# One gather of 256 columns for the first two expert pairs of a layer, in place of two of 128

## The chip, the cores and the metric

The kernel runs on one NeuronCore of a Trainium2 chip. The metric is device time in microseconds (us) of one execution, the median of several. The engines are TensorE (matmuls, "PE"; its weight loads are shown apart as "PEld"), VectorE ("DVE"), ScalarE ("ACT"), GpSimdE ("POOL") and SyncE ("SP"), whose queue issues the DMAs that bring the weights.

## What is computed

The reference is a transformer of two layers over 256 tokens of `x` and 256 tokens of context, width 1024. Each layer has a mixer (a gated recurrence and spatial gating in layer 0, latent attention in layer 1) and then a mixture of 32 experts, of which each token takes two. Layer 0 sends 512 tokens to its experts, layer 1 only the 256 of `x`. For each expert:

```
g, u = split(xb @ w_gu[e])          # xb: the rows of the tokens that chose e; w_gu 1024 x 1024
y    = (silu(g) * u) @ w_dn[e]      # w_dn 512 x 1024
out[token] += weight[token, e] * y
```

## The kernel before

Everything that the change touches is in `moe`, which runs once in each layer. An expert has 64 places (`CAP`), and two experts make a pair, so a layer has 16 pairs; `step(p)` does one pair. Tokens are brought to places by matmuls with one-hot matrices. `one_hots(g)` makes, in one VectorE instruction, the matrix `P` for two pairs at once: 256 columns, the first 128 for the even pair and the last 128 for the odd one. `gather` (L871) multiplies the token rows, kept as a high and a low part in fp32r, by `P`: for each of 8 blocks of 128 features it issues one matmul for each token tile and part. That is 8 x 8 = 64 matmuls in layer 0 (`NT` = 4 token tiles) and 8 x 4 = 32 in layer 1 (`NT` = 2), each with as many columns as the `P` that it was given. The products land in PSUM tiles named `ad` (3 buffers of 512 columns: 4 blocks at 128 columns, 2 at 256) and ACT and DVE copy them to `xT`.

The order of TensorE's work in the expert loop is that of the source (`manual_schedule`). In `step(p)` it is: `gate_up` of the first expert and of the second (L916, 64 matmul records in a step, of 512 columns in fp32, two of them side by side in the array), then a filler, then `turned` (L935, transposes of the hidden rows), then the rest of the filler, `back` (L901, transposes of the weights of the places) and `down` (L1027, 32 records). Between the last matmul of `gate_up` and `turned` stands `hidden` (L920), a chain of ACT and DVE instructions; the filler is what TensorE does meanwhile. It is:

- for an odd pair: the gather of the next two pairs, of 256 columns;
- for a later even pair: `combine` (L1046), which adds the results of the pairs before to the tokens;
- for pair 0: the gather of the second half of `P`, 128 columns, that pair 1 will need. The first half was gathered ahead of the loop, and `R.blocks` (L309, some tiny matmuls) follows it.

After pair 11 of layer 0 and pair 5 of layer 1 (`MID`) all results so far are combined and every engine takes a branch (`tc.If`, L1179) round a loop for overfull experts. The step after it, an even one, finds nothing to combine: its filler is empty.

Each pair needs 12 loads of 1 MB, issued by SP in order (`load_to`, L849) into a ring of 13 buffers in layer 0 and 17 in layer 1. A load waits until the matmuls that read the old content of its buffer are done. The ring is full when a layer's first gather starts.

Of the kernel before, what the change touches and what calls it, by code (L numbers as in the profile page):

```python
# [25 lines left out]
def body(ctx, tc, I, out, dbg=None, stop=None):  # L26
# [783 lines left out]
    def moe(R, wxa, nwb, out=None):  # L810
# [5 lines left out]
        with ExitStack() as st:  # L816
# [16 lines left out]
            def load_to(n):  # L833

                for i in range(len(loads), min(n, n_load)):
                    p, j = divmod(i, 12)
                    e, j, src = (2 * p + j // 4, j % 4, I["moe_w_gu"]) if j < 8 else (2 * p + (j - 8) // 2, j % 2, I["moe_w_dn"])
                    w = turn[i % len(turn)].tile([128, 2, D], F32, name="w")
                    if i >= n_load - 4:

                        c = (i - n_load + 4) // 2
                        v = w.rearrange("p k (h n) -> p (k h) n", h=2)
                        for e in range(2):
                            nc.sync.dma_start(v[:, 2 * e:2 * e + 2],
                                              src[l, NE - 2 + e, j * 256:(j + 1) * 256, c * 512:(c + 1) * 512]
                                              .rearrange("(p k) n -> p k n", p=128))
                        loads.append(v)
                        continue
                    nc.sync.dma_start(w, src[l, e, j * 256:(j + 1) * 256, :].rearrange("(p k) n -> p k n", p=128))  # L849
                    loads.append(w)  # L850
# [10 lines left out]
            def weigh(P, b, weights):  # L861

                a = weights.shape[2]
                n = 128 // a
                Pw = mo.tile([128, NT, 128], F32, name="z", bufs=4)
                V.tensor_tensor(Pw.rearrange("p t (a n) -> p t a n", a=a),
                                P[:, :, 128 * b:128 * b + 128].bitcast(F32).rearrange("p t (a n) -> p t a n", a=a),
                                weights[:, :, :, None].to_broadcast([128, NT, a, n]), op=OP.mult)
                return Pw

            def gather(P, xT, q0=0, q1=4):  # L871

                n = P.shape[2]
                m = 512 // n
                for cb in range(2 * q0 // m, 2 * q1 // m):
                    px = Q("ad", (128, m, n))
                    for j in range(m):
                        k = cb * m + j
                        for i in range(2 * NT):
                            t, part = divmod(i, 2)  # L880
                            mm(px[:, j, :], hs[t][:, part, 256 * (k // 2) + k % 2:256 * (k // 2) + 256:2], P[:, t, :],  # L881
                               start=i == 0, stop=i == 2 * NT - 1)
                    if R.mod is None:
                        if cb % 2:
                            act(xT[:, cb * m:cb * m + m], px, AF.Copy)
                        else:
                            V.tensor_copy(xT[:, cb * m:cb * m + m], px)
                        continue
                    for j in range(m):
                        k = cb * m + j  # L890
                        S, A = [R.mod[:, g, k:k + 1] for g in range(2)]
                        if j % 2:
                            act(xT[:, k], px[:, j], AF.Identity, scale=A, bias=S)
                        else:
                            V.tensor_scalar(xT[:, k], px[:, j], A, S, op0=OP.mult, op1=OP.add)

            def back(Pw):

                pt = Q("bt", (128, 4, 128))
                for t in range(NT):  # L900
                    tp(pt[:, t, :], Pw[:, t, :], ident)  # L901
                ws = mo.tile([128, 1], F32, name="ws", bufs=2)
                act(junk_of(NT * 128), pt[:, 0:NT, :].rearrange("p t n -> p (t n)"), AF.Copy, accum_out=ws)
                PT = mo.tile([128, NT, 128], F32R, name="PT", bufs=2)
                V.tensor_scalar(PT, pt[:, 0:NT, :], 0.0, None, op0=OP.is_gt)
                return PT, ws

            def gate_up(xT, base, wg):

                gu = Q("gu")  # L910
                for j in range(4):
                    w_ = wg(j)
                    for k in (2 * j, 2 * j + 1):
                        w = w_[:, k % 2, :].rearrange("p (a c n) -> p c a n", a=2, c=2)
                        for c in range(2):
                            mm(gu[64 * c:64 * c + 64, :], xT[:, k, base:base + CAP], w[:, c],  # L916
                               start=k == 0, stop=k == KC - 1)
                return hidden(gu)
# [37 lines left out]
            def total(z, t, c, pend):  # L956

                mm(z, ident, xs[t][:, c * 512:(c + 1) * 512], start=True, stop=False, skip_group_check=True)  # L958
                for y, PT in pend:
                    for part in range(2):  # L960
                        mm(z, PT[:, t, :], y[c][:, part], start=False, stop=False, skip_group_check=True)  # L961
# [150 lines left out]
            def one_hots(g):  # L1112
                return onehots(cm[:, :, 4 * g:4 * g + 4], iota[:, 0:CAP])

            def rows_tile():
                return mo.tile([128, 8, 256], F32, name="xT", bufs=1)

            def step(p):

                nonlocal xT, P  # L1120
                load_to(12 * p + 12)
                w = loads[12 * p:12 * p + 12]
                odd = p % 2
                more = odd and p < last
                b = 128 * odd
                Pw = weigh(P, odd, wsel[:, :, 2 * p:2 * p + 2])
                if more:
                    P = one_hots((p + 1) // 2)
                end = p == last and out is not None
                h = [gate_up(xT, b, lambda j: w[j])]  # L1130
                if end:
                    z = [[None] * 2 for _ in range(2)]
                    for c, t in ((0, 0), (0, 1), (1, 0)):
                        z[t][c] = Q("ad")
                        total(z[t][c], t, c, pend)
                    PT, ws = back(Pw)
                h.append(gate_up(xT, b + CAP, lambda j: w[4 + j]))
                n = 2 * NT
                if more:
                    xT = rows_tile()  # L1140
                    gather(P, xT, 0, 3)
                elif end:
                    z[1][1] = Q("gu")
                    total(z[1][1], 1, 1, pend)
                elif p == 0:
                    gather(P[:, :, 128:256], xT[:, :, 128:256])
                else:
                    combine(pend, 0, n - 1)
                hT = turned(h)
                if end:  # L1150
                    finish(hT, w[8:], PT, ws, fg, z)
                    return
                if more:
                    gather(P, xT, 3, 4)
                else:
                    combine(pend, n - 1, n)
                    pend.clear()
                PT, ws = back(Pw)
                if p < last:
                    gated = p == last - 1 and out is not None  # L1160
                    pend.append((down(hT, lambda j: (w[8 + j], w[10 + j]), ws, gated), PT))
                else:
                    settle(hT, w[8:], PT, ws)

            P = one_hots(0)
            with tc.manual_schedule(engines=pes):
                xT = rows_tile()
                gather(P[:, :, 0:128], xT[:, :, 0:128])
                R.blocks(mo, Q)
                for p in range(MID[l] + 1):  # L1170
                    step(p)
                combine(pend)
                pend.clear()
# [253 lines left out]
    with ExitStack() as main:  # L1427
        HL = main.enter_context(tc.tile_pool(name="hl", bufs=1))
        wst, wxa, R = even_layer(HL, main)
        if stop != "even":  # L1430
            moe(R, wxa, 4)
        wst.close()
# [3 lines left out]
    with ExitStack() as main:  # L1436
        HL = main.enter_context(tc.tile_pool(name="hl1", bufs=1, side="right", reuse_waits="tile"))
        R = odd_layer(HL, main)
        moe(R, wxa, 4, out)
# [40 lines left out]
```

## Time and profile before

| | |
|---|---|
| median of 3 runs | 1553.11 us (1551.04 to 1554.37) |
| the profiled execution | 1554.18 us, its span 1552.4 us |
| PE busy | 1459.8 us (94%) |
| DVE, ACT, POOL busy | 664.9, 434.0, 225.3 us |
| mean granted TensorE clock | 0.966 of full speed |
| moved by DMA | 495.24 MB, 319 GB/s over the span |

The durations of the rows below come from the profiled execution. The span runs from the first to the last instruction, and 1.8 us of the execution lie around it. The clock is given as a share of 2.4 GHz: 1.00 is 2.4 GHz and 0.50 is 1.2 GHz; a mean between the two says which share of a stretch was at which.

### The profile page before, as it was taken

The page shows a single profiled execution, that of the slowest core. Times are in us where ns is not written, and L with a number is a line of the kernel's source. Part 1 is how long each engine was busy: PE and PEld are TensorE (multiplying, and loading weights), DVE is VectorE, ACT ScalarE, POOL GpSimd, SP SyncE. Part 2 cuts the span into 40 slices and gives each one's busy share as a digit, 9 for nine tenths or more (in the row PEclk, how much of TensorE's full clock was granted, in tenths as well). Part 3 has the DMA queues.
Part 4 walks back from the last instruction along what each step waited for, and adds up shares of the span by engine and source line. Part 5 has one row for each costly group of instructions (what it writes and reads, how often), then busy time and mean ns, then how long its engine had stood idle before and what let it go on. Part 6 is the DMA issues. An engine that isn't in the chain of part 4 may idle for free. (4 is left out here: it accounts for less than half of the span.)

```text
span 1552.4 us, 21816 instructions
## 1 busy us (share of the span) xinstructions
PE 1459.8 (94%) x8622; PEld 857.8 (55%) x8622; DVE 664.9 (43%) x1498; ACT 434.0 (28%) x988; POOL 225.3 (15%) x250
## 2 busy tenths in 40 slices
PE   7999999998999999999999988997999989989987
PEld 5777777867644554554535356786344434444443
DVE  4555556758224334244413455576232332322222
ACT  4433334623121121111112144453222212212212
POOL 2321212133002112012203221101010100010010
PEclk9999999998799999999999989997999999999999
DMA  9774434885899999999999853125999999999994
GB/s 356 232 256 143 156 120 161 299 318 192 320 372 420 420 420 420 420 420 420 382 376 382 321 216 112 43 96 204 372 420 420 420 419 421 420 420 421 420 420 191
DMA packets 126052, 495.24 MB, mean 319 GB/s; under 512 B 17739, under 2 KB 38636, under 8 KB 77816
## 3 DMA queue, kind: packets, MB, share of 16 engines
q1 hardware_dynamic: 119704, 487.33, 79.6%
q10 hardware_dynamic: 2192, 3.72, 0.7%
q0 software_dynamic: 4048, 2.73, 0.6%
q8 instruction: 71, 1.16, 0.3%
q14 instruction: 37, 0.30, 0.1%
HBM read 492.59 MB, written 1.13 MB: 318 GB/s over the span
## 5 line engine op out<-in xcount | busy, mean ns | idle before, releaser
L916 PE MATMUL gu<-w,xT 128*64 128x512 f32 x2048 | 462.9, 604 | 18.0 <-DMA w<-in_moe_w_gu_dram 13.2
L916 PEld LDWEIGHTS gu<-w,xT 128*64 128x64 f32 x2048 | 153.3, 139 | 316.9 <-issue 278.5
L1027 PE MATMUL dn<-w,hh 128*64 128x512 f32 x960 | 219.5, 604 | 0.0
L924 DVE COPY hh<-gu 128x256 f32<-128x256 f32 x64 | 27.2, 425 | 371.3 <-ACT junk L923 371.3
L1050 POOL TENSOR_TENSOR xx<-xx,z 128x512 f32<-128x512 f32 x56 | 72.9, 1324 | 767.4 <-DVE z L1049 767.4
L1027 PEld LDWEIGHTS dn<-w,hh 128*64 128x64 f32 x960 | 76.1, 139 | 121.9 <-issue 112.3
L923 ACT ACTIVATE junk<-gu 128x256 f32<-128x256 f32 x64 | 24.6, 384 | 401.7 <-PE gu L916 401.7
L120 PE MATMUL mm<-WH,hH 128*128 128x512 f32 x288 | 116.7, 407 | 0.8 <-ACT hH L115 0.7
L121 PE MATMUL mm<-WL,hH 128*128 128x512 f32 x288 | 115.2, 400 | 1.4 <-DVE WL L116 1.4
L122 PE MATMUL mm<-WH,hL 128*128 128x512 f32 x288 | 112.5, 400 | 0.0
L1017 DVE SCALAR_TENSOR_TENSOR y<-dn,ws,y 128x512 fp32r<-128x512 f32 x60 | 45.0, 751 | 145.7 <-ACT y L1016 143.6
L1046 PE MATMUL ad<-y,PT 128*128 128x512 f32 x368 | 94.8, 404 | 5.3 <-DVE z L1049 4.1
L1016 ACT ACTIVATE y<-dn,ws 128x512 fp32r<-128x512 f32 x60 | 41.2, 687 | 176.1 <-PE dn L1027 165.6
L1046 PEld LDWEIGHTS ad<-y,PT 128*128 128x128 f32 x368 | 66.0, 188 | 36.1 <-issue 13.0
L115 ACT ACTIVATE WH<-w 128x512 fp32r<-128x512 f32 x80 | 48.4, 627 | 107.6 <-PE mm L122 86.0
L116 DVE TENSOR_TENSOR WL<-w,WH 128x512 fp32r<-128x512 f32 x76 | 56.6, 752 | 50.9 <-ACT WH L115 49.4
L1049 DVE TENSOR_TENSOR z<-ad,gt 128x512 f32<-128x512 f32 x100 | 66.1, 683 | 13.3 <-PE ad L1046 10.2
L881 PE MATMUL ad<-P,hH 128*128 128x256 f32 (+1 forms) x288 | 63.0, 302 | 1.5 <-DVE P L856 1.5
L120 PEld LDWEIGHTS mm<-WH,hH 128*128 128x128 f32 x288 | 54.9, 191 | 16.9 <-issue 3.8
L399 PE MATMUL ad<-w,cst 128*32 128x128 f32 x1536 | 59.3, 280 | 5.1 <-DMA w<-in_ada_w_dram 5.0
L121 PEld LDWEIGHTS mm<-WL,hH 128*128 128x128 f32 x288 | 54.8, 190 | 13.1 <-DVE WL L116 1.5
L122 PEld LDWEIGHTS mm<-WH,hL 128*128 128x128 f32 x288 | 54.5, 191 | 13.2 <-issue 1.6
(434 smaller groups left out, 1989.3 us busy)
## 6 DMA issues: line engine op xcount, KB each, us to landing
w<-in_moe_w_gu_dram SPq DMA_DIRECT2D x256, 1024.0 KB, 16.3
w<-in_moe_w_dn_dram SPq DMA_DIRECT2D x120, 1024.0 KB, 12.0
w<-in_ada_w_dram SPq DMA_DIRECT2D x48, 1024.0 KB, 7.4
w<-in_ev_w_in_dram SPq DMA_DIRECT2D x32, 256.0 KB, 4.6
w<-in_moe_w_dn_dram SPq DMA_DIRECT2D x16, 512.0 KB, 11.2
w<-in_ev_w_in_dram SPq DMA_DIRECT2D x6, 1024.0 KB, 5.1
w<-in_ev_w_out_dram SPq DMA_DIRECT2D x4, 1024.0 KB, 6.8
w<-in_od_w_out_dram SPq DMA_DIRECT2D x4, 1024.0 KB, 5.0
```

The lines of the kernel that those rows point to most:

```text
L115: act(H, src, AF.Copy)
L116: (eng or V).tensor_tensor(L, src, H, op=OP.subtract)
L120: mm(out, lh, rh, start=start, stop=False, skip_group_check=True)
L121: mm(out, lh, rl, start=False, stop=False, skip_group_check=True)
L122: return mm(out, ll, rh, start=False, stop=stop, skip_group_check=True)
L399: mm(pa[32 * j:32 * j + 32, 0:128], cst[:, k, :], w[k // 4][:, k % 4, j * 128:(j + 1) * 128], start=k == 0, stop=cols is not None and k == ...
L881: mm(px[:, j, :], hs[t][:, part, 256 * (k // 2) + k % 2:256 * (k // 2) + 256:2], P[:, t, :], start=i == 0, stop=i == 2 * NT - 1)
L916: mm(gu[64 * c:64 * c + 64, :], xT[:, k, base:base + CAP], w[:, c], start=k == 0, stop=k == KC - 1)
L1027: mm(py[c][64 * par:64 * par + 64, :], hT[par][:, k // 2, k % 2, :], w_[par][:, k % 2, c * 512:(c + 1) * 512], start=k == 0, stop=k == 3)
L1046: mm(cb, PT[:, t, :], y[c][:, i % 2], start=i == 0, stop=i == 2 * len(pend) - 1)
L1049: V.tensor_tensor(z, cb, gate[t // 2][:, hs_], op=OP.mult)
L1050: (V if n % 4 == 3 else nc.gpsimd).tensor_tensor(xs[t][:, hs_], xs[t][:, hs_], z, op=OP.add)
```

## The change

The first gather of a layer now takes the whole of `P`: as many matmuls as one of the two gathers before, each with 256 columns. The gather in pair 0's step goes. As `pend` is empty there, the `combine` that now stands in its branch does nothing, and pair 0's filler is empty.

```diff
@@ in step(p)
                 elif end:
                     z[1][1] = Q("gu")
                     total(z[1][1], 1, 1, pend)
-                elif p == 0:
-                    gather(P[:, :, 128:256], xT[:, :, 128:256])
                 else:
                     combine(pend, 0, n - 1)
                 hT = turned(h)
@@ ahead of the loop
             P = one_hots(0)
             with tc.manual_schedule(engines=pes):
                 xT = rows_tile()
-                gather(P[:, :, 0:128], xT[:, :, 0:128])
+                gather(P, xT)
                 R.blocks(mo, Q)
                 for p in range(MID[l] + 1):
                     step(p)
```

## Rows read from the trace of the kernel before

**Rows 1.** Stretches: length, busy us of PE, PEld, DVE, ACT, POOL; clock, DMA share, GB/s.

```profile
400.00:440.00 40.00, 39.25 (x213) 20.24 (x214) 9.17 (x19) 6.31 (x14) 0.00 (x0) 0.94 0.73 289
440.00:760.00 320.00, 318.62 (x1664) 159.64 (x1658) 118.28 (x195) 62.17 (x143) 40.93 (x30) 1.00 1.01 420
1108.00:1114.00 6.00, 6.00 (x30) 2.01 (x28) 0.85 (x2) 1.37 (x2) 0.00 (x0) 1.00 0.81 306
1114.00:1500.00 386.00, 364.11 (x1738) 163.50 (x1736) 113.18 (x234) 81.64 (x194) 27.45 (x21) 0.99 1.01 420
```

**Rows 2.** PE's waits, 402 to 892 us (all): us in total, times, longest.

```profile
PE ad L1046 <- DVE z L1049: 4.1, 10, 1.2
PE gu L916 <- DVEq L1179: 2.2, 1, 2.2
PE bt L935 <- DVE hh L927: 2.1, 1, 2.1
PE bt L901 <- ACT hh L939: 1.5, 2, 0.7
```

**Rows 3.** Timeline of PE, layer 0, pair 0: start, us, instructions [idle before].

```profile
402.69 15.09 PE L916 MATMUL gu<-w,xT 128*64 128x512 f32 x64
417.70 0.45 PE L881 MATMUL ad<-P,hH 128*128 128x128 f32 x2
...
427.34 7.09 PE L1027 MATMUL dn<-w,hh 128*64 128x512 f32 x32
434.26 3.17 PE L916 MATMUL gu<-w,xT 128*64 128x512 f32 x14
```

**Rows 4.** Stretches, the gather's matmuls (L881) alone: PE busy, clock, DMA.

```profile
388.69:402.43 13.74, 13.73 (x64) 0.50 0.75 310
417.70:425.30 7.60, 7.60 (x64) 1.00 1.01 423
744.63:750.51 5.88, 5.88 (x48) 1.00 1.01 417
1077.37:1084.26 6.89, 6.89 (x32) 0.50 0.06 20
```

**Rows 5.** Stretches of three `gate_up` pairs (pairs 0 and 12; layer 1, pair 0).

```profile
402.69:417.70 15.01, 15.01 (x67) 4.70 (x64) 2.99 (x9) 1.78 (x4) 0.00 (x0) 0.92 0.73 267
771.13:787.94 16.81, 16.81 (x64) 5.62 (x64) 4.58 (x8) 1.22 (x3) 0.84 (x1) 0.82 0.97 365
1084.47:1099.93 15.46, 15.46 (x67) 4.80 (x65) 3.53 (x11) 2.13 (x5) 0.00 (x0) 0.90 0.68 278
```

**Rows 6.** Timeline of PE, layer 0, pair 11 of pairs 0 to 15.

```profile
730.79 13.90 PE L916 MATMUL gu<-w,xT 128*64 128x512 f32 x64
744.63 0.52 PE L881 MATMUL ad<-P,hH 128*128 128x256 f32 x2
```

**Rows 7.** Timeline of PE, the two steps with an empty filler.

```profile
787.94 0.51 PE L935 MATMUL bt<-ident,hh 128*128 128x128 f32 x2
...
802.12 13.90 PE L916 MATMUL gu<-w,xT 128*64 128x512 f32 x64
...
1264.01 0.51 PE L935 MATMUL bt<-ident,hh 128*128 128x128 f32 x2
...
1268.18 8.78 PE L1027 MATMUL dn<-w,hh 128*64 128x512 f32 x32
1276.80 13.90 PE L916 MATMUL gu<-w,xT 128*64 128x512 f32 x64
```

**Rows 8.** Loads issued from 700 to 714 us, and us from issue to landing.

```profile
L849 SPq DMA_DIRECT2D w<-in_moe_w_gu_dram x8: 327/328/383, 701.7 to 713.3; - x8
...
DMA to landing us min/median/max: 14.8/15.9/17.9
```

**Rows 9.** Timeline of SP, layer 1: the first loads after the stop.

```profile
1088.03 3.76 SPq L849 DMA_DIRECT2D w<-in_moe_w_gu_dram  x3
```

**Rows 10.** Timeline of PE, layer 1, pair 0.

```profile
1105.97 7.09 PE L1027 MATMUL dn<-w,hh 128*64 128x512 f32 x32
```

## The prediction

> **What bounds the kernel now.** I read the slices first, to see which stage is bound by what, then the waits of TensorE, then the timeline round the first gather, and last the clock of each stretch. The expert loops of the two layers have different bounds.
>
> In layer 0 TensorE is the bound. From 440 to 760 us it is busy for 318.62 of 320.00 us, and the DMA engines are busy too (1.01, 420 GB/s) [rows 1]. Two full resources: the waits tell them apart. In all that TensorE waited for between 402 and 892 us there is no DMA [rows 2]. The weights come early: the eight loads issued from 701.7 to 713.3 us landed at most 17.9 us later, by 731.2 us, while the last of them is read in the last eighth of a `gate_up` pair that starts at 730.79 us and takes 13.84 us, so from 742.9 us: a lead of 11.7 us [rows 6, 8]. The DMA engines aren't full from the start: between 400 and 440 us their share is 0.73, so 10.8 us of their time went by while the ring waited for TensorE [rows 1]. So what shortens TensorE's path in layer 0 shortens the kernel, and what frees buffers earlier also feeds the loads earlier.
>
> In layer 1 the loads are the bound. From 1114 to 1500 us the DMA share is 1.01, and TensorE is busy for 364.11 of 386.00 us [rows 1]. During the first gather the DMA engines stand nearly still (0.06) [rows 4]: the ring is full. The first load after that is issued at 1088.03 us [rows 9], when the first eighth of `gate_up` has freed a buffer. From there on the loads need a fixed time to the end, so here the moment of that restart counts, and little else.
>
> The clock is the third thing to see. Both first gathers run wholly at 0.50 [rows 4]. Before them TensorE had waited for the routing. Through 13.74 us of matmuls back to back in layer 0, and 6.89 us in layer 1, the clock did not rise; it rose soon after `gate_up` had begun. The mean clock of that `gate_up` pair tells when: 0.92 over 15.01 us is 2.4 us at half speed, and 0.90 over 15.46 us is 3.1 us. After the branch, `gate_up` starts at half speed once more, and 0.82 over 16.81 us is 6.0 us [rows 5].
>
> **The price of a wide matmul.** At 1.00 a gather matmul of 128 columns takes 7.60 / 64 = 0.119 us and one of 256 takes 5.88 / 48 = 0.1225 us: twice the columns at 3% more. At 0.50 the narrow one takes 13.73 / 64 = 0.2145 us [rows 4]. No row shows a wide one at 0.50. Its floor is the narrow one's 0.2145; twice the narrow one, 0.429, is its ceiling; the wide one's own time at half the clock, 0.245, is the nearest row. The narrow one came out below its doubled time (0.2145 for 0.238), so I take 0.2145, and keep 0.245 for the range.
>
> The Trainium skill, page "TensorE: Matmul & The Clock Gate", section "Back-to-back issue gap", has the isolated spacing grow with the columns, N/1.2 ns at the low clock and N/2.4 + 2.5 ns at the high one. By that rule one wide gather would cost as much as two narrow ones, and the sum would be left with a loss of cover alone. The trace disagrees for these fp32r matmuls.
>
> **The change, part by part.** First, the gather ahead of the loop in layer 0: 64 matmuls, now of 256 columns. Its evacuations carry the same elements in all, and move ahead of the loop; a chunk of 512 columns takes 16 matmuls before and after it is copied, and there are three buffers, so TensorE does not wait for them. What matters is the clock. I expect that wide matmuls bring it up as `gate_up` does, within the same time: the three rows give 2.4, 6.0 and 3.1 us, mean 3.8 [rows 5]. At 0.2145 us, 17.7 matmuls are done in 3.8 us, and the other 46.3 at 0.1225 take 5.67: 9.5 us instead of 13.74 [rows 4], a gain of 4.3 us (4.9 with 2.4 us, 3.3 with 6.0 us).
>
> Second, pair 0's `gate_up` then starts at full clock: 13.84 us [rows 6] for 15.01 [rows 5], a gain of 1.2 us.
>
> Third, the gather in pair 0's step goes, and with it the cover of `hidden`. Before, from the end of `gate_up` to the start of the next one were 434.26 - 417.70 = 16.56 us [rows 3]. After, the step is like the two whose filler is empty. They took 802.12 - 787.94 = 14.18 us and 1276.80 - 1264.01 = 12.79 us [rows 7]: gains of 2.4 and 3.8 us. Part of these steps ran at half clock, since the clock fell behind the stall: `down` took 8.62 us in the second of them [rows 7] and takes 434.26 - 427.34 = 6.92 at full clock [rows 3]. If the clock holds, the step is 4.17 us of stall [rows 7] and 6.92, and the gain 5.5 us. I take the mean of the two seen, 3.1 us (2.4 to 5.5). Layer 0 gains 4.3 + 1.2 + 3.1 = 8.6 us.
>
> Does it last? The leads shrink by at most 8.6 us of 11.7, and by less, since the buffers come free earlier too while the ring still waits. Behind the loop the combine and the mixer of layer 1 hang on TensorE's results, and I take them to move as a whole.
>
> Fourth, layer 1: 32 matmuls, 17.7 in the first 3.8 us and 14.3 at 0.1225, 1.76 us: 5.6 for 6.89 [rows 4], a gain of 1.3 us (1.9 or 0.4). The buffer for the restart comes free after an eighth of `gate_up`: 1088.03 - 1084.47 = 3.56 us before [rows 5, 9], 13.84 / 8 = 1.73 at full clock [rows 6], a gain of 1.8. The restart comes 3.2 us earlier (2.2 to 3.8), and the end with it.
>
> Fifth, pair 0's `down` in layer 1 frees four buffers. It starts 1105.97 - 1099.93 = 6.04 us behind `gate_up` [rows 5, 10] and after the change 4.17 [rows 7], 1.9 us earlier, which could fill the hole that the DMA engines have from 1108 to 1114 us (0.81 of 6 us, 1.1 us lost) [rows 1]; at half clock `down` gives that back. I take 0.5 us (0 to 1.1).
>
> DMAs, SP's queue and the one-hot instructions stay as they were. The sum is 8.6 + 3.2 + 0.5 = 12.3 us. From the profiled execution's 1554.18 us it leaves 1541.9; the median of the runs is 1.1 us lower than that execution, which would leave 1540.8. I predict 1541.5.
>
> **The rivals.** A (0.65) is the forecast: 9.1 to 16.5 us off, 1537 to 1545.
>
> B (0.20): the wide gather doesn't raise the clock, as the narrow one did not. For it: 13.74 us at 0.50 without a rise [rows 4]. Against it: the wide ones stream twice the columns in the same time. Then only the third and fifth terms stay: 3.1 + 0.5 = 3.6 us, 1550.6; at 0.245 us for the wide ones another 2.0 and 1.0 us are lost, 1553.6.
>
> The same page of the Trainium skill, section "What's actually happening", says that activity releases the throttle and that instructions are not counted. By that rule the kind of matmul would not matter, the clock terms would fall away and B would be left. For the narrow gather the trace disagrees: it is active throughout and the clock stays at 0.50.
>
> C (0.07): layer 0's gain is lost because its loads, whose engines are full [rows 1], become the bound. Against it stand the leads above. Layer 1's 3.7 us remain: 1550.5.
>
> D (0.05), the other side: at half clock the wide matmul costs in proportion to its columns, and the clock stays low. At 0.429 us the gathers grow by 13.7 and 6.9 us, less the 3.6 of B: 17.0 us slower, 1571.2. It decides from 0.2145 + 3.6 / 96 = 0.252 us on. Against it: the full-clock rows, 0.1225 to 0.119 [rows 4].
>
> The remaining 0.03 is for clock falls elsewhere that undo the gain.
>
> **Numbers.** A measurement tells about 0.2% from no change, 3.1 us. Faster: all of A, most of C, half of B: 0.82. Same: the rest of B and C with some of the remainder, 0.10. Slower: D, a little of B and the remainder, 0.08. The range reaches from A's lower end to B and C, 1537 to 1551; it leaves out D and B's dear end.
>
> **What would show it.** Right: the first gathers are one block of 64 and 32 wide matmuls, some 9.5 and 5.6 us long, the clock rises inside them, `gate_up` of pair 0 takes 13.8 us, a stall of some 4.2 us stands in pair 0's step, layer 0 ends 8 to 9 us earlier, and the loads restart 3 us earlier against the gather's start. Wrong: a clock of 0.50 up to `gate_up`, a wide matmul above 0.25 us, DMA among TensorE's waits in layer 0, or a gain in layer 0 that is gone when layer 1's gather starts.

## The result, and the profile after

The changed kernel takes 1537.95 us (median of 4 runs, 1536.51 to 1541.76); the kernel before takes 1552.88 us beside it. The ratio is 0.9905, with a 95% interval of [0.9887, 0.9923], which makes 14.8 us less; the gains of whole runs below are worked out from their ratios in the same way. The forecast was 1541.5 us, a gain of 11.6 us. The profiled execution took 1538.64 us. The first part of its page:

```profile
span 1536.9 us, 21613 instructions
...
PE 1435.8 (93%) x8526; PEld 836.2 (54%) x8526; DVE 662.7 (43%) x1494; ACT 432.5 (28%) x984; POOL 224.9 (15%) x250
```

TensorE is busy for 24.0 us less than in the table before; between the second profiles of the two kernels (below) it is 16.0 us (1452.3 and 1436.3), so a part of the 24.0 is scatter. Where it went is read from the same views. First the gather's matmuls alone, in stretches cut where the clock rises (length, PE busy, clock, DMA share, GB/s):

```profile
392.77:396.40 3.63, 3.63 (x17) 0.50 0.94 364
396.50:402.17 5.67, 5.67 (x49) 1.00 1.01 422
...
1067.51:1072.20 4.69, 4.69 (x22) 0.50 0.10 31
...
1067.51:1073.61 6.10, 6.10 (x32) 0.61 0.08 24
```

They answer to [rows 4]. The wide gather starts at half clock (0.50, which is 1.2 GHz) as the narrow one did, but the clock comes up inside it, 3.7 us after its start in layer 0 and 4.7 us in layer 1. At half clock a wide matmul takes 4.69 / 22 = 0.213 us, as a narrow one does. Next the timeline of PE round pair 0 of layer 0, against [rows 3]:

```profile
402.36 13.95 PE L916 MATMUL gu<-w,xT 128*64 128x512 f32 x64
416.25 0.51 PE L935 MATMUL bt<-ident,hh 128*128 128x128 f32 x2
418.81 0.51 PE L935 MATMUL bt<-ident,hh 128*128 128x128 f32 x2 [2.06 <-DVE hh L927]
420.07 0.90 PE L901 MATMUL bt<-ident,z 128*128 128x128 f32 x4 [0.75 <-ACT hh L939]
420.89 8.49 PE L1027 MATMUL dn<-w,hh 128*64 128x512 f32 x32
429.21 2.31 PE L916 MATMUL gu<-w,xT 128*64 128x512 f32 x10
```

The stretches of `gate_up` and of `down` (columns as in [rows 1]):

```profile
402.36:416.25 13.89, 13.89 (x68) 4.51 (x65) 4.63 (x11) 1.81 (x4) 0.00 (x0) 1.00 0.86 337
420.89:429.21 8.32, 8.32 (x33) 2.69 (x34) 0.69 (x1) 1.27 (x3) 0.00 (x0) 0.83 0.90 352
```

`gate_up` takes 416.25 - 402.36 = 13.89 us, all at full clock. Then the cover is gone: TensorE waits 2.06 us for the hidden rows (DVE L927). The 0.75 us that it waits for the PSUM tile that `turned` and `back` share (ACT L939) are no part of the change: they stand twice in [rows 2], and twice after. `down` takes 8.32 us up to 429.21 instead of 6.92, at a mean clock of 0.83: the clock fell behind the stall.

In layer 1 the same, on PE (against [rows 10]) and on SP's queue (against [rows 9]):

```profile
1073.70 13.96 PE L916 MATMUL gu<-w,xT 128*64 128x512 f32 x64
1087.59 0.51 PE L935 MATMUL bt<-ident,hh 128*128 128x128 f32 x2
...
1091.78 7.09 PE L1027 MATMUL dn<-w,hh 128*64 128x512 f32 x32
```

```profile
1075.68 3.76 SPq L849 DMA_DIRECT2D w<-in_moe_w_gu_dram  x3
```

The loads restart 1075.68 - 1067.51 = 8.17 us after the gather's start; before it was 1088.03 - 1077.37 = 10.66. Here the stall left the clock alone: `down` starts 4.19 us behind `gate_up` and runs at full speed. In the second profile of the changed kernel the clock fell in both layers, and `down` took 8.61 us in each. Whole stretches, against [rows 1], and all that PE waited for from 402 to 890 us, against [rows 2]:

```profile
400.00:440.00 40.00, 37.19 (x180) 14.18 (x180) 10.28 (x23) 6.97 (x16) 0.00 (x0) 0.96 0.94 380
440.00:760.00 320.00, 318.67 (x1659) 161.60 (x1656) 120.77 (x197) 62.10 (x141) 43.21 (x32) 1.00 1.01 420
...
1092.00:1104.00 12.00, 12.00 (x58) 4.02 (x56) 1.93 (x3) 1.79 (x4) 0.00 (x0) 1.00 1.01 415
1104.00:1490.00 386.00, 364.03 (x1738) 161.11 (x1734) 112.50 (x233) 81.56 (x194) 27.42 (x21) 0.99 1.01 420
```

```profile
PE ad L1046 <- DVE z L1049: 4.2, 11, 1.2
PE bt L935 <- DVE hh L927: 4.1, 2, 2.1
PE gu L916 <- PEq L1177: 3.2, 1, 3.2
PE bt L901 <- ACT hh L939: 1.5, 2, 0.7
PE ad L1046 <- DVE y L1017: 0.9, 1, 0.9
```

Layer 0 is still TensorE's: no DMA among the waits. The hole that the loads had from 1108 to 1114 us, 20 us behind their restart, is gone in this profile (1.01 in the stretch where it would stand).

Two profiles of one kernel differ in places that the change does not touch, so both kernels were profiled twice. The table gives stretches in us, from the starts that the four timelines show:

| stretch | before | before, again | after | after, again |
|---|---|---|---|---|
| start to layer 0's first gather | 388.7 | 392.1 | 392.8 | 391.4 |
| gather to pair 1's `gate_up` | 45.6 | 45.4 | 36.4 | 37.3 |
| to `gate_up` behind the branch | 336.9 | 336.9 | 337.9 | 338.3 |
| to layer 1's first gather | 306.2 | 299.2 | 300.4 | 305.7 |
| gather to the loads' restart | 10.7 | 10.7 | 8.2 | 7.6 |
| restart to the end | 464.4 | 464.6 | 461.2 | 463.7 |
| span | 1552.4 | 1548.9 | 1536.9 | 1543.9 |

Rows two and five are the change; they scatter by less than 1 us within a kernel. Rows one and four, which the change does not touch, differ by 3.4 and 7.0 us between the two profiles of the kernel before, and by 1.4 and 5.3 us between those of the changed one.

### The profile page after: what moved, and what is told of

It is laid out like the page before. It is cut to its first block, busy times and chain, and to the rows that moved or that the text cites. A ratio compares the mean times of both kernels' runs of the same rounds, so it can differ in the third digit from the quotient of the medians.

```text
span 1536.9 us, 21613 instructions
## 1 busy us (share of the span) xinstructions
PE 1435.8 (93%) x8526; PEld 836.2 (54%) x8526; DVE 662.7 (43%) x1494; ACT 432.5 (28%) x984; POOL 224.9 (15%) x250
## 5 line engine op out<-in xcount | busy, mean ns | idle before, releaser
L916 PE MATMUL gu<-w,xT 128*64 128x512 f32 x2048 | 456.6, 597 | 19.1 <-DMA w<-in_moe_w_gu_dram 13.2
L414 POOL DMA_DIRECT2D mod<-ada_r x80 | 40.4, 512 | 140.1 <-ACT ada_r L412 126.0
```

## The experiments

### Whose gain is it: the gather that went, or the wider one?

First, the wide gather with the second one kept as cover:

```diff
+                elif p == 0:
+                    gather(P[:, :, 128:256], xT[:, :, 128:256])   # again, as cover
...
                 gather(P, xT)
```

> The first gather is the wide one, and pair 0's step still gathers the second half of the places, which it already has: work done twice, as cover alone. Theory (wide matmuls bring the clock up): the first gather takes 9.4 us in layer 0 and 6.1 us in layer 1 as in the changed kernel, gate_up of pair 0 13.9 us, and pair 0's step 16.6 us as before the change. Gain 5.6 us in layer 0 and some 2.5 us in layer 1, in all 8 us: ratio about 0.995. Rival (the gain is the TensorE time of the gather that went, less a stall): nothing went, so the ratio is 1.000 or a little above.

Measured: ratio 0.9945 [0.9928, 0.9961]. The gather's stretches:

```profile
392.25:401.51 9.26, 9.26 (x64) 0.82 1.00 391
415.50:423.30 7.80, 7.71 (x64) 1.00 1.01 420
```

With as much work as before, and wider matmuls in it, 8.5 us come off. The rival falls: more than half of the gain is had without taking a matmul away.

Second, the reverse: no wider matmul, the second narrow gather ahead of the loop behind the first.

```diff
+                gather(P[:, :, 0:128], xT[:, :, 0:128])
+                gather(P[:, :, 128:256], xT[:, :, 128:256])
-                gather(P, xT)
```

> Both narrow gathers stand ahead of the loop, none in pair 0's step, and no matmul is wider. Theory: the clock stays at 0.50 through both, 128 matmuls at 0.2145 us, 27.5 us in layer 0 and 13.8 us in layer 1, so layer 0 loses 13.7 us ahead of the loop and gets 3 us back in pair 0's step, and layer 1's loads restart 6.9 us later: some 17 us slower than before the change, ratio 1.011. Rival (TensorE busy for long enough brings the clock up, whatever its matmuls are; 13.7 us was just too short): the clock rises inside the 27.5 us, and the loss is 10 us or less, ratio 1.006 or less.

Measured: ratio 1.0131 [1.0114, 1.0148], 20 us slower. The two gathers together, in layer 0 and in layer 1:

```profile
392.38:419.74 27.36, 27.36 (x128) 0.50 0.39 157
1087.11:1100.84 13.73, 13.73 (x64) 0.50 0.03 10
```

For 27.36 us TensorE multiplies back to back, and the clock stays at 1.2 GHz. The rival that busy time alone brings it up is out. The Trainium skill, page "TensorE: Matmul & The Clock Gate", section "What's actually happening", lets activity release the throttle and does not count instructions. If activity is read as busy time, this trace disagrees for narrow fp32r matmuls.

The loss is 3 us more than the 17 expected. The two stretches that the edit owns lose what was expected: from the gather to pair 1's `gate_up` 55.96 us for 45.56, and from layer 1's gather to the restart 17.65 for 10.66, 17.4 us together. Where the other 3 us lie stays open.

Third, can a narrow gather run at full clock at the start of a layer? The kernel before, with other matmuls right ahead of its first gather:

```diff
                 xT = rows_tile()
+                pw = Q("gu")
+                for i in range(6):
+                    mm(pw, ident, xs[0][:, 0:512], start=True, stop=True, skip_group_check=True)
                 gather(P[:, :, 0:128], xT[:, :, 0:128])
```

> The kernel before the change, with six unread matmuls (identity by a token tile, 512 columns of fp32) in TensorE's order right ahead of each first gather, so that nothing else stands between them and the narrow gather. Read from the profile, not from the time: they delay the gather by some 5 us. Theory (the clock has to be brought up by other work, and a narrow gather then keeps it): the clock rises within the unread matmuls, the narrow gather runs at 1.00, 7.6 us for 13.7 in layer 0 and 3.9 us for 6.9 in layer 1, and gate_up of pair 0 takes 13.9 us. Rival (narrow matmuls at a layer's start run at half clock whatever came before): the clock falls to 0.50 again inside the gather, and gate_up starts at half clock.

One execution took 1550.11 us. The stretches of the added matmuls up to the clock's rise, of the narrow gather, and of `gate_up`:

```profile
388.10:393.50 5.40, 5.40 (x11) 2.30 (x10) 2.91 (x7) 0.00 (x0) 0.54 (x1) 0.50 0.97 360
...
395.60:403.60 8.00, 8.00 (x66) 7.77 (x64) 0.69 (x1) 0.00 (x0) 0.00 (x0) 1.00 0.63 264
403.85:417.70 13.85, 13.85 (x67) 4.49 (x64) 2.99 (x9) 1.80 (x4) 0.00 (x0) 1.00 0.76 293
```

The 512-column matmuls bring the clock up, and the narrow gather behind them runs at 1.00, 8.0 us for 13.7; in layer 1 likewise, 4.05 us for 6.89. So in this profile a narrow gather keeps the clock that it finds; at a layer's start it finds the low one.

A lighter form of this failed. It gave the kernel before two or three such matmuls in the routing and one ahead of the gather, for the wait for the one-hot matrix:

```diff
+            if t1 == self.NT:
+                pw = Q("mm")
+                for i in range(3 if l else 2):
+                    mm(pw, ident, xs[0][:, 0:512], start=True, stop=True, skip_group_check=True)
             prk = Q("bt", (128, 4, 32))
...
+                mm(Q("gu"), ident, xs[0][:, 0:512], start=True, stop=True, skip_group_check=True)
                 gather(P[:, :, 0:128], xT[:, :, 0:128])
```

> The kernel before the change, narrow gathers and all, with matmuls whose product nobody reads (identity by a token tile, 512 columns of fp32): two in layer 0 and three in layer 1 while TensorE waits for the last routing, and one while it waits for the one-hot matrix. Theory (the gain of the first gather is the clock's, and a narrow gather keeps the clock but doesn't raise it): the clock is up when the gather starts, the narrow ones take 0.119 us, the first gather 7.6 us in layer 0 and 3.9 us in layer 1, gate_up of pair 0 13.9 us: 7.3 us off in layer 0 and some 4.5 us in layer 1, ratio about 0.992, with no wide matmul. Rival (a first gather of narrow matmuls runs at half clock whatever came before, or the waits are too short to matter): clock 0.50 through the gather, ratio 1.000.

Measured: ratio 1.0017 [1.0005, 1.0029], where 0.992 was expected. TensorE's order in the routing is a scheduler's, and it put the added matmuls from 369 us on, well ahead of the wait that they were for. One alone stood right ahead of the gather, the clock was low, and the narrow gather left it so:

```profile
392.11:405.82 13.71, 13.68 (x64) 0.50 0.73 297
```

The same additions in front of the wide gather:

> The changed kernel with the same unread matmuls in TensorE's waits ahead of the first gather. Theory: no part of the wide gather is left at half clock, 7.8 us for 9.4 in layer 0 and 3.9 us for 6.1 in layer 1, so 1.6 us and about 2.2 us less than the changed kernel: ratio to before about 0.988. Rival (the unread matmuls delay the routing's own matmuls by what they save): no better than the changed kernel, 0.9905.

Measured: ratio 0.9930 [0.9914, 0.9946], where 0.988 was expected: no better than the changed kernel. Behind the same single matmul the wide gather does reach the high clock, and takes 8.60 us:

```profile
388.10:396.70 8.60, 8.57 (x64) 0.89 1.01 415
```

Up to the end of the first gather those two differ in its width alone, and confirm the cause; as a way to gain time the additions are useless where they landed.

### One layer at a time

```diff
-                elif p == 0:
+                elif p == 0 and l != 0:      # l != 1 in the second
                     gather(P[:, :, 128:256], xT[:, :, 128:256])
...
+                if l == 0:                   # l == 1 in the second
+                    gather(P, xT)
+                else:
+                    gather(P[:, :, 0:128], xT[:, :, 0:128])
```

> The change in layer 0 alone; layer 1 keeps its two narrow gathers. Theory: layer 0's gain, 4.4 + 1.2 + 3.5 = 9 us, passes through the mixer of layer 1 to the end: ratio about 0.994. Rival (layer 0's loads take its gain back, or layer 1's loads do not start from it): ratio 0.998 to 1.000.

> The change in layer 1 alone; layer 0 keeps its two narrow gathers. Theory: only the earlier restart of the loads counts, 2.5 to 3.2 us, and up to 1 us of the hole behind pair 0's step: ratio about 0.9975. Rival (layer 1 gains as layer 0 does, by all the TensorE time saved, 1 + 1.6 + 2): 5 us or more, ratio 0.9965 or less; and the other rival (its loads hide everything): 1.000.

Measured: 0.9959 [0.9945, 0.9972] for layer 0 alone, 6.4 us, and 0.9979 [0.9964, 0.9993] for layer 1 alone, 3.3 us. The gathers of layer 0 and layer 1 in the first kernel, and then in the second:

```profile
391.02:400.16 9.14, 9.14 (x64) 0.83 1.00 393
1069.83:1076.72 6.89, 6.89 (x32) 0.50 0.07 23
```

```profile
393.74:407.46 13.72, 13.72 (x64) 0.50 0.66 267
1074.53:1080.40 5.87, 5.87 (x32) 0.62 0.05 17
```

Each layer answers to its own gather. Layer 0 alone gains less than the 9 us expected: from the gather to pair 1's `gate_up` it saves 45.56 - 36.12 = 9.4 us, PE's wait at the branch gives back 0.9 (3.04 us for 2.17), and the 8.5 us that are left are the far end of the interval (4.3 to 8.5 us). No DMA stands among its PE waits from 402 to 860 us, so nothing shows the loads taking the gain back. Layer 1's gain is about as large as its restart's (1082.52 - 1074.53 = 7.99 us for 10.66, 2.7 us); its interval reaches to 0.9964 and does not quite shut out the rival's 0.9965. Together they give 0.9959 x 0.9979 = 0.9938, some 0.002 either way, which lies above the interval of the result (up to 0.9923) though its own reaches into it; so both kernels were run again.

### The same kernels again

> The kernel before, unchanged, as a second profile: ratio 1.000. Its first gathers should run wholly at 0.50 again, 13.7 and 6.9 us; the clock's falls elsewhere, and the time up to the first gather, may stand differently, and show how far two profiles of one kernel differ by 2 to 4 us for no reason of the change.

> The changed kernel again, as a second profile and a second ratio: 0.9905 as the first time if what the terms leave over (2 to 3 us, behind the branch and in the tail) comes with the change, 0.992 (the 12.3 us of the sum) if it came from where the clock happened to fall in the first profiles. The two layers changed one at a time give 0.9938 together, which speaks for the latter.

Measured: 0.9999 [0.9987, 1.0011] for the kernel before, and 0.9923 [0.9910, 0.9935] for the changed one: 12.0 us, at the sum's 12.3 and the forecast's 11.6. The two intervals overlap, and the 14.8 of the first measurement may have a share of chance. For single executions the table shows where such a share can lie: the first profile of before had the slowest passage behind the branch, the first of after one of the faster ones. Some 39 us from `gate_up` on behind the branch, for before, before again, after, after again:

```profile
771.13:810.13 39.00, 36.20 (x142) 12.53 (x144) 8.66 (x17) 5.54 (x13) 0.84 (x1) 0.84 0.93 369
```

```profile
774.40:813.00 38.60, 35.75 (x166) 13.77 (x168) 9.54 (x19) 6.37 (x15) 0.89 (x1) 1.00 1.01 411
```

```profile
767.13:806.13 39.00, 36.20 (x162) 13.28 (x164) 9.43 (x19) 6.37 (x15) 0.00 (x0) 0.96 0.99 406
```

```profile
767.00:806.00 39.00, 36.20 (x144) 12.50 (x146) 8.93 (x18) 5.79 (x14) 0.00 (x0) 0.84 0.92 378
```

The stretches begin with the same instructions and hold the same stalls, with a mean clock from 0.84 to 1.00, and 142 to 166 TensorE instructions get done in them. From that `gate_up` to the next one it is 30.99, 25.57, 26.89 and 30.61 us, a large part of the scatter in row four. The kernel before shows both ends, so these falls are no effect of the change.

### What the stall in pair 0's step costs

Unread matmuls as a filler, where the filler is empty:

```diff
+                elif not pend:
+                    pw = Q("ad")
+                    for i in range(2):
+                        mm(pw, ident, xs[0][:, 0:512], start=True, stop=True, skip_group_check=True)
                 else:
                     combine(pend, 0, n - 1)
```

> The changed kernel with two unread matmuls of 512 columns in fp32 (0.85 us each at full clock) as the filler of the steps whose filler is empty: pair 0 and the pair behind the branch. Theory (the stall there costs its 4.2 us, and on top of it the clock, which falls behind it): the clock stays at 1.00 through down, 6.9 us for 8.3, some 1.5 us off at each such place in layer 0, and at layer 1's little, since its loads set the end: ratio to before about 0.988. Rival (the fall is not due to the stall, or costs nothing): 0.9905 as the changed kernel.

> The changed kernel with two unread matmuls as the filler of the empty steps, a second time, since its first ratio, 0.9895, lay between the changed kernel's two, 0.9905 and 0.9923, and a hair below. If the held clock is worth its 1.6 us in pair 0's step and as much behind the branch where the clock falls there, the ratio is again 0.990 or less, 1.5 to 3 us below the changed kernel; if the first one was where the clock happened to fall elsewhere, it is 0.992.

Measured: 0.9895 [0.9878, 0.9912] and 0.9900 [0.9879, 0.9920]. The timeline of PE in pair 0's step, first profile:

```profile
415.37 1.98 PE L1148 MATMUL ad<-xx,ident 128*128 128x512 f32 x4
...
417.94 0.50 PE L935 MATMUL bt<-ident,hh 128*128 128x128 f32 x2 [0.36 <-DVE hh L927]
...
419.78 7.09 PE L1027 MATMUL dn<-w,hh 128*64 128x512 f32 x32
426.69 3.60 PE L916 MATMUL gu<-w,xT 128*64 128x512 f32 x16
```

`down` takes 426.69 - 419.78 = 6.91 us and the step 11.3 us (from 415.37) instead of 12.96: the 1.6 us of the fallen clock come back, the stall itself stays (`down` starts 419.78 - 415.37 = 4.41 us behind `gate_up`). It repeats: behind pair 0 of both layers and behind the branch of layer 0, `down` takes 6.91 or 6.92 us in all six places of the two profiles, while in the two profiles of the changed kernel it takes 8.3 to 9.0 us in five of the six. Both ratios lie below both of the changed kernel (0.9905, 0.9923), but the intervals overlap: this is probably the best version here, by some 1 to 4 us, and the runs do not settle by how much.

Real work in the stall did not do as well. `back` needs nothing of the hidden rows:

```diff
+                first = not more and not end and not pend
+                if first:
+                    PT, ws = back(Pw)
                 hT = turned(h)
...
-                PT, ws = back(Pw)
+                if not first:
+                    PT, ws = back(Pw)
```

> The changed kernel, but in the steps whose filler is empty the transposes of the weights of the places (back, 2 or 4 matmul records) go ahead of turned, into the stall, where they can run since they need nothing of hidden. Theory (the stall of pair 0 is hidden's chain and then the one PSUM tile that turned and back share): the 0.75 us that back waits behind turned and its own 0.4 to 0.6 us go, so each such step is some 1 us shorter, the ratio to before about 0.990 and no more than 2 us below the changed kernel. Rival (back's own ACT and DVE work then stands in the way of hidden's or of turned's tile): the step is as long as before or longer.

Measured: 0.9948 [0.9935, 0.9961], slower than the changed kernel. The timeline of PE:

```profile
416.19 0.66 PE L901 MATMUL bt<-ident,z 128*128 128x128 f32 x4
420.26 0.75 PE L935 MATMUL bt<-ident,hh 128*128 128x128 f32 x4 [3.42 <-DVE PT L905]
421.48 8.79 PE L1027 MATMUL dn<-w,hh 128*64 128x512 f32 x32 [0.47 <-ACT hh L939]
```

`back` and `turned` share one PSUM tile, and `turned` now waits 3.42 us for it, until DVE has read `back`'s product (L905), behind the work on the hidden rows. `down` starts 5.3 us behind `gate_up` (421.48 - 416.19) instead of 4.6. The rival was right for the step: it is longer. But this is 0.7 us, and the kernel is 4 to 7 us slower than the changed one; the rest was not traced.

## Why the prediction was right

**The bounds.** TensorE for layer 0, the loads for layer 1: this fits the layers one at a time and the waits after. The loads' time from restart to end, taken as fixed, was so only within 3.4 us (461.2 to 464.6 in the table).

**The price of the wide matmul.** Taken as 0.2145 us at half clock, measured 0.213. Rival D, a price in proportion to the columns, falls with it. The Trainium skill, page "TensorE: Matmul & The Clock Gate", section "Back-to-back issue gap", gives N/1.2 ns at the low clock for the isolated spacing, which is 213 ns for 256 columns: the trace agrees for the wide one, and not for the narrow one, which takes the same.

**The clock.** That wide matmuls raise it was an analogy to `gate_up`, and it held. It rose 3.7 us after the gather's start in layer 0 where 3.8 was taken, and 4.7 us in layer 1; in the second profile it rose after 5.4 and some 3.5 us. The rows behind the 3.8 went from 2.4 to 6.0 us, so the first profile's nearness to it is luck. The start of pair 0's `gate_up` came 9.59 us after the gather's for 13.99: 4.4 us for the 4.3 predicted, 3.6 in the second profile; in the seven profiles with the wide gather and nothing added ahead of it, it comes after 9.3 to 10.4 us. `gate_up` gave 1.1 us for 1.2. Rival B falls with the stretches of the wide gather and the first two experiments.

**Pair 0's step.** 12.96 us (429.21 - 416.25) for 16.56, 3.6 us where 3.1 was taken and 2.4 to 5.5 allowed (3.5 in the second profile). Its parts are as told: the stall, and a clock that falls behind it or doesn't. The stall was taken as 4.17 us, from a row of layer 1, where `back` has two transposes; in layer 0 it has four, and `down` started 4.64 and 4.41 us behind `gate_up`.

**Layer 0 in sum.** 8.6 us predicted, 9.1 and 8.1 us measured from the gather to pair 1's `gate_up` in the two profiles. A piece was missed: PE's wait at the branch grew from 2.2 to 3.2 and 3.6 us (below), which leaves 8.1 and 6.8 us up to the `gate_up` behind it. Rival C falls: in none of the profiles does a DMA stand among PE's waits from 402 to 860 us.

**Layer 1.** Predicted 3.2 us for the restart, measured 2.5 and 3.1. In the first profile the gather gave 0.9 us for 1.3, as the clock rose later than taken, and the first eighth of `gate_up` 1.6 for 1.8. Behind the restart 0.5 us was taken for a hole that would be filled. The runs do not show this term: the hole is filled in the first profile (1.01), nearly so in the second (0.94), and not with the change in layer 1 alone (0.77), and in the chain that ended last the last load lands 401.1, 403.5 and 402.5 us behind the restart in these three, for 402.6 and 402.8 in the two profiles of before. What both profiles of the changed kernel do have is a tail, from that landing to the end, of 60.1 us for 61.8, where no term of the sum stands. It goes with the clock (0.80 in the last pair's first `gate_up` for 0.73 and 0.74), and not with the gather: the second and third experiment, with narrow gathers, have 60.1 us, and the first, with the wide one, 61.7.

**The time.** The sum was 12.3 us; two measurements give 14.8 and 12.0. The median of 1537.95 us lies inside the forecast's own range, near its lower end. That the sum stands so near the second measurement is in part luck: it left out PE's longer wait at the branch (1.0 and 1.4 us lost) and the shorter tail (1.6 us won), which nearly cancel, and its fifth term is not shown. It also had no term for the scatter of the clock's falls, 5.4 us in the step behind the branch.

## What to carry to other kernels

Read the clock of a stage before its instructions: 13.7 us of work that looked bound by its matmuls was bound by a clock that those matmuls never raised, and doing twice the columns in each made the whole stage shorter. In this kernel, after a wait on TensorE it paid to begin with the wider matmuls, and to leave narrow fp32r ones to a clock that is up. Before a gain is put down to an edit, profile both kernels twice: the stretches that the edit owns repeat within 1 us here, and others move by up to 7.

## What was not expected of the hardware

In the gathers, in fp32r, 128 columns cost what 256 do, at either clock (0.119 and 0.1225 us, 0.2145 and 0.213), and a stream of 128-column matmuls keeps a high clock (7.6 us at 1.00) but did not raise a low one in 27.36 us. Each of these matmuls has a weight load of its own (PEld). The narrow gather before and the start of the wide one after, with the columns of [rows 1]:

```profile
388.70:402.40 13.70, 13.70 (x64) 13.70 (x64) 1.97 (x3) 0.00 (x0) 0.54 (x1) 0.50 0.75 311
392.80:396.35 3.55, 3.55 (x16) 3.55 (x17) 1.25 (x2) 0.00 (x0) 0.25 (x1) 0.50 0.93 359
```

In both the weight loads are busy throughout, where in `gate_up` they take 4.51 of 13.89 us. That they set the price, and so make it the same for both widths, fits these rows; no run tests it.

PE's wait at the branch behind pair 11 is 2.17 to 2.18 us in the five profiles whose expert loop of layer 0 has as many TensorE instructions as before (the two of before, the first two experiments, layer 1 alone), and 3.0 to 3.6 us in the nine other profiles, whether they have more or fewer. In the five the profile names DVE's sequencer as what ended the wait, in the nine PE's own. The DMA queues that carry instructions tell the two groups apart as well. Their packets within that wait (768.96 to 771.13 us before, then 763.91 to 767.13 us after; packets, MB, share):

```profile
q8 instruction: 1, 0.02, 2.6%
```

```profile
q8 instruction: 1, 0.02, 2.2%
q14 instruction: 1, 0.01, 1.0%
```

All nine longer waits hold the second packet, on q14, 0.4 to 1.0 us before `gate_up` starts; none of the five shorter ones does. So the longer wait goes with a load of instructions that then falls into it. That TensorE waits for this packet is likely, and not tested; it costs the change 1.0 and 1.4 us in its two profiles.
